# Attention scores of the first block: second product over 128 rows, keys' low parts kept in the gate rows' buffers

## Chip, cores and metric

One core of a Trainium2 chip runs the whole program in one launch. The metric is the device time of that core in microseconds (us); lower is better. All times of instructions are from one profiled execution of the kernel before.

## What is computed

Two transformer blocks are run one after the other on 256 latent tokens and 256 context tokens of width 1024. The change is in the first block, which has two layers. Each layer is: a feed-forward sublayer, an attention sublayer, a second feed-forward sublayer. Layer 0 has neighbourhood attention (16 heads of 64, each query sees a window of latent keys and all 256 context keys; the context queries are computed too). Layer 1 has windowed attention with 16 query heads on 4 key heads and a sink logit, for latent queries only. What matters here is the product of queries and keys:

```
s_win = jnp.einsum('bcqhd,bicjhd->bhcqij', q_r, k_r).astype(jnp.float32) + bias
s_ctx = jnp.einsum('bcqhd,bkhd->bhcqk', q_r, kc).astype(jnp.float32)
p = jax.nn.softmax(jnp.concatenate([s_win, s_ctx], axis=-1), axis=-1)
```

with head dimension 64 and 512 keys (256 latent, 256 context).

## The kernel before

Products keep nearly full float32 precision by splitting each operand into a high part (rounded to the fast fp32r type) and a low part (what the rounding left). A projection is three products into one accumulator, at lines 247, 248 and 249 (`mm3`): high by high, high by low, low by high.

Two heads of 64 share the 128 rows (partitions) of one projected tile; a head's rows are `ROWS[j]` (line 842). `head_parts` (line 845) makes the operands of the scores from such a tile. For the queries it makes one tile per head: the head's own 64 rows hold the high part (ScalarE, line 861), the other head's 64 rows hold this head's low part (VectorE, line 867). For the keys it makes one tile per head with the high part twice, once in each half (ScalarE, lines 861 and 864), and one tile `lo` for both heads with the low parts, each head on its own 64 rows (VectorE, line 865).

`attend_rows` (line 871) computes the scores; its `dot` is two matmuls into one PSUM bank: line 878 over all 128 rows, which is (query high + query low) by key high, and line 879 over the head's 64 rows alone, which is query high by key low. A head pair of layer 0 has four such dots against 512 keys (latent queries) and four against 256 keys (context queries), with 8 head pairs; a pair of layer 1 has four dots against 512 keys, again with 8 pairs. That makes 64 + 32 = 96 dots.

After the scores come `softmax_rows` (line 788: VectorE maximum at lines 805, 810 and 815, ScalarE exponential at 819, VectorE scaling at 828), `transpose_probs` (line 832: TensorE transposes at 838, ScalarE copies at 839) and the product with the values at line 914, whose output tile is 64 columns wide per head, so that its matmuls use the array as 128 rows by 64 columns.

`neighborhood` (line 944) goes over head pairs: project the next pair's queries and keys (`project_qk`, 48 matmuls), finish the current pair (`finish`: transposes and values), score the next (`score`). `window` (line 1054) does the same with queries alone (24 matmuls a pair, `project_tile`), since its two key tiles are made once; there each projected tile goes through a rotation (`roped`, line 1076) first. Instructions are written in this order per engine; a scheduler at build time interleaves them where they don't depend on each other, and each engine then runs its own list strictly in order.

The gate rows: `gate_rows` (line 443) loads a row of 1024 numbers, spread over 128 partitions, into the buffers `gate0` (latent) and `gate1` (context), by two DMAs of GpSimd's queue (line 449). The last reader before attention is the residual of the feed-forward sublayer (line 569); `close_attention` (line 1032) loads the next gates for the residual after attention. Both buffers idle between. In layer 1 only `gate0` is loaded by `close_attention`, since the context isn't needed any more.

`e.zeros` (line 358) is a tile of 256 columns of zeros that is there already.

Of the kernel before, what the change touches and what calls it, by code (L numbers as in the profile page):

```python
# [11 lines left out]
F32R = mybir.dt.float32r  # L12
BF16 = mybir.dt.bfloat16
AF = mybir.ActivationFunctionType
ALU = mybir.AluOpType
AX = mybir.AxisListType.X

P = 128
D = 1024
KT = D // P  # L20
NT = 512
HALF = 256
# [819 lines left out]
ROWS = [slice(0, 64), slice(64, 128)]  # L842


def head_parts(e, pool, src, tag, scale, keys, bufs=1):

    V, S, nm = e.V, e.S, e.nm
    n = int(src.shape[-1])

    def tile(i):
        return pool.tile([P, n], F32R, tag=f"{tag}{i}", bufs=bufs, name=nm("hp"))

    hi = [tile(j) for j in range(2)]
    lo = tile(2) if keys else None
    for j in range(2):
        r, o = ROWS[j], ROWS[1 - j]  # L860
        S.activation(hi[j][r], src[r], AF.Copy, scale=scale)
        h = hi[j][r].bitcast(F32)
        if keys:
            S.copy(hi[j][o], hi[j][r])
            V.tensor_tensor(lo[r], src[r], h, ALU.subtract)
        else:
            V.scalar_tensor_tensor(hi[j][o], src[r], scale, h, ALU.mult, ALU.subtract)  # L867
    return hi, lo


def attend_rows(e, pool, q, k, bias, sinks, with_ctx):

    T = e.T
    kh, kl = k

    def dot(b, j, qc, kc):
        r = ROWS[j]
        T.matmul(b, q[j][:, qc], kh[j][:, kc], start=True, stop=False)  # L878
        T.matmul(b, q[j][r, qc], kl[r, kc], start=False, stop=True)  # L879

    lat, sk = [], []
    for j in range(2):
        for qt in range(2):
            b = e.bank("S")
            dot(b, j, slice(qt * P, qt * P + P), slice(0, NT))
            lat.append((b, bias(j, qt)))
            sk.append(sinks(j) if sinks else None)
    jobs = [(softmax_rows(e, pool, lat, sk if sinks else None), 0, 4)]
    if with_ctx:
        ctx = []  # L890
        for j in range(2):
            b = e.bank("S").rearrange("p (a b) -> p a b", a=2)
            for qt in range(2):
                c0 = HALF + qt * P
                dot(b[:, qt], j, slice(c0, c0 + P), slice(HALF, NT))
                ctx.append((b[:, qt], None))
        jobs.append((softmax_rows(e, pool, ctx), 2, 2))
    return jobs
# [21 lines left out]
def head_outputs(e, pool, n, last):  # L920

    oh, ol = e.uh_ul
    kept = pool.tile([P, last, n], F32, name=e.nm("kept"))

    def split(k, o):
        e.S.activation(oh[:, k, :n], o, AF.Copy)
        e.V.tensor_tensor(ol[:, k, :n], o, oh[:, k, :n].bitcast(F32), ALU.subtract)  # L930

    def take(k, o):
        if k < last:
            e.V.tensor_copy(kept[:, k], o)
            return
        if k == last:
            for i in range(last):
                split(i, kept[:, i])
        split(k, o)

    return take


def neighborhood(e, rest):
    nc, a, V, S, G, T, nm, per = e.nc, e.a, e.V, e.S, e.G, e.T, e.nm, e.per
    uh, ul = e.uh_ul
    with ExitStack() as st:
        pool = e.pool(nm("na"), st)
        take = head_outputs(e, pool, NT, KT - 2)

        def lhs(k, t):
            return uh[:, k, t * P : t * P + P], ul[:, k, t * P : t * P + P]

        def values(dh):
            v = [pool.tile([P, 512], F32, tag=f"v{t}", name=nm("v")) for t in range(4)]
            e.project(
                e.wunits(a["nav"][dh], KT, 2), lhs, range(4),
                lambda t, y: S.copy(v[t], y),
            )
            return v  # L960

        vals, qks, rows = {}, {}, {}

        def qk_weights(hp):
            return [
                e.split(e.raw(a["naqk"][hp, :, i * D : (i + 1) * D], (KT, P)))
                for i in range(2)
            ]

        def products(b, w, c):  # L970
            for k in range(KT):
                e.mm3(b[:, c], w[0][:, k], w[1][:, k], uh[:, k, c], ul[:, k, c],
                      k == 0, k == KT - 1)

        def close_qk(hp, bs):
            q = head_parts(e, pool, bs[0], "q", 0.125, False)[0]
            qks[hp] = q, head_parts(e, pool, bs[1], "k", 1.0, True)

        def project_qk(hp):
            ws = qk_weights(hp)  # L980
            bs = [e.bank("B") for _ in range(2)]
            for i in range(2):
                products(bs[i], ws[i], slice(0, NT))
            close_qk(hp, bs)

        def score(hp):
            bt = e.fb[0].tile([P, 2, 2, HALF], F32, tag=f"lnr{hp % 2}", name=nm("nab"))
            for rq in range(4):
                nc.scalar.dma_start(
                    bt[64 * (rq % 2) : 64 * (rq % 2) + 64, rq // 2],  # L990
                    a["nabias"][:, 2 * hp : 2 * hp + 2, 3 - rq : 7 - rq],
                )
            q, k = qks.pop(hp)
            rows[hp] = attend_rows(e, pool, q, k, lambda j, qt: bt[:, qt, j], None, True)

        def finish(hp):
            o = e.bank("O")
            attend_values(
                e, rows.pop(hp), vals[hp // 4],
                lambda j: slice((2 * (hp % 4) + j) * 64, (2 * (hp % 4) + j) * 64 + 64), o,  # L1000
            )
            take(hp, o)

        lead = []
        for hp in range(2):
            ws = qk_weights(hp)
            bs = [e.bank("L") for _ in range(2)]
            for i in range(2):
                products(bs[i], ws[i], slice(0, HALF))
            lead.append((ws, bs))  # L1010
        for hp, (ws, bs) in enumerate(lead):
            for i in range(2):
                products(bs[i], ws[i], slice(HALF, NT))
            if hp == 0:
                close_qk(0, bs)
        vals[0] = values(0)
        rest()
        score(0)
        for hp in range(KT):
            if hp == 0:  # L1020
                close_qk(1, lead[1][1])
            elif hp + 1 < KT:
                project_qk(hp + 1)
            if hp == 4:
                vals[1] = values(1)
            finish(hp)
            if hp + 1 < KT:
                score(hp + 1)
    return close_attention(e, 0, a["nao"], uh, ul, range(4))
# [24 lines left out]
def window(e, rest):  # L1054
    nc, a, V, S, G, T, nm, per = e.nc, e.a, e.V, e.S, e.G, e.T, e.nm, e.per
    uh, ul = e.uh_ul
    with ExitStack() as st:
        pool = e.pool(nm("wa"), st)
# [17 lines left out]
        def roped(b, n):  # L1076
            t = e.dn[0].tile([P, NT], F32, tag="rt", bufs=2, name=nm("roped"))[:, :n]
            S.copy(t, b[:, :n])
            rb = e.bank("R")
            T.matmul(rb[:, :HALF], rot, t[:, :HALF], start=True, stop=True)  # L1080
            tmp = pool.tile([P, HALF], F32, tag="rtmp", bufs=2, name=nm("rtmp"))
            V.tensor_tensor(tmp, rb[:, :HALF], rope[:, 1], ALU.mult)
            V.tensor_tensor(t[:, :HALF], t[:, :HALF], rope[:, 0], ALU.mult)
            V.tensor_tensor(t[:, :HALF], t[:, :HALF], tmp, ALU.add)
            return t

        ks, qs, rows = [], {}, {}

        def tile_weights(m):
            on = G if m >= 4 else V  # L1090
            return e.split(e.raw(a["waqk"][m // 2, :, (m % 2) * D : (m % 2 + 1) * D], (KT, P)), on)

        def products(b, w, c):
            for k in range(KT):
                e.mm3(b[:, c], w[0][:, k], w[1][:, k], uh[:, k, c], ul[:, k, c],
                      k == 0, k == KT - 1)

        def project_tile(m):
            w = tile_weights(m)
            b = e.bank("B")  # L1100
            products(b, w, slice(0, HALF))
            qs[m - 2] = head_parts(e, pool, roped(b, HALF), "q", 0.125, False, 2)[0]

        def score(i):
            rows[i] = attend_rows(
# [12 lines left out]
        lead = {}  # L1118
# [3 lines left out]
        for m in range(2):  # L1122
            w, b = lead[m]
            products(b, w, slice(HALF, NT))
        for m in range(2):
            qs[m] = head_parts(e, pool, roped(lead[2 + m][1], HALF), "q", 0.125, False, 2)[0]
        e.project(e.wunits(a["wav"], KT, 4), lhs, range(4), evac)
        rest()
        for m in range(2):
            ks.append(head_parts(e, pool, roped(lead[m][1], NT), f"k{m}", 1.0, True))  # L1130
        score(0)
        for i in range(KT - 2):
            project_tile(i + 4)
# [695 lines left out]
```

## Time and profile before

| | |
|---|---|
| three runs, median (lowest to highest) | 2608.67 us (2604.34 to 2611.02) |
| profiled execution, own time | 2611.17 us |
| its span, first to last instruction | 2609.0 us |
| TensorE busy | 2437.8 us (93%) |
| VectorE, ScalarE, GpSimd busy | 1677.8 (64%), 834.6 (32%), 138.1 (5%) us |
| mean granted clock of TensorE | 0.976 |

Busy is the time in which an engine has an instruction in work. TensorE's matmuls are pipelined and their ends are modelled: a matmul that starts while the one ahead is still in work is shown overlapping it, so what tells the pace is the time from one start to the next. A matmul comes with a load of its stationary operand (LDWEIGHTS, shown as engine PEld).  A shape such as 64*128 behind a matmul is the part of the array that it uses, rows by columns.

### The profile page before, as it was taken

The page shows a single profiled execution, that of the slowest core. Times are in us where ns is not written, and L with a number is a line of the kernel's source. Part 1 is how long each engine was busy: PE and PEld are TensorE (multiplying, and loading weights), DVE is VectorE, ACT ScalarE, POOL GpSimd, SP SyncE. Part 2 cuts the span into 40 slices and gives each one's busy share as a digit, 9 for nine tenths or more (in the row PEclk, how much of TensorE's full clock was granted, in tenths as well). Part 3 has the DMA queues.
Part 4 walks back from the last instruction along what each step waited for, and adds up shares of the span by engine and source line. Part 5 has one row for each costly group of instructions (what it writes and reads, how often), then busy time and mean ns, then how long its engine had stood idle before and what let it go on. Part 6 is the DMA issues. An engine that isn't in the chain of part 4 may idle for free.

```text
span 2609.0 us, 33471 instructions
## 1 busy us (share of the span) xinstructions
PE 2437.8 (93%) x12930; PEld 1772.0 (68%) x12930; DVE 1677.8 (64%) x3134; ACT 834.6 (32%) x1412; POOL 138.1 (5%) x151
## 2 busy tenths in 40 slices
PE   8999999999999999999999998999998999798865
PEld 5888888676888888888887768997665422455211
DVE  5978856645899764997985778877744322564211
ACT  3322224645322221322222564444432100443000
POOL 0000000000000000000000200001101000210000
PEclk9999999999999999999999999999998999998987
DMA  8766623222277763576653326875127899536998
GB/s 322 265 198 201 192 77 115 65 81 96 93 253 243 240 227 122 179 235 200 216 180 101 95 81 208 303 235 170 51 81 296 343 427 422 201 104 253 428 427 337
DMA packets 118847, 545.46 MB, mean 209 GB/s; under 512 B 15008, under 2 KB 21408, under 8 KB 106656
## 3 DMA queue, kind: packets, MB, share of 16 engines
q1 hardware_dynamic: 104256, 517.25, 55.5%
q10 hardware_dynamic: 10368, 12.37, 1.6%
q0 software_dynamic: 4064, 13.70, 1.5%
q8 instruction: 102, 1.67, 0.3%
q14 instruction: 57, 0.47, 0.1%
HBM read 542.15 MB, written 1.11 MB: 208 GB/s over the span
## 4 chain that ended last, share of the span: by engine, by line
PE 80%; DMA 7%; DVE 7%; ACT 2%; POOL 2%; issue 2%; ACTq 0%; SPq 0%; POOLq 0%; DVEq 0%
PE pB L247 12%; PE pB L248 12%; PE pB L249 12%; PE pA L249 7%; PE pA L247 7%; PE pA L248 7%; PE pA L1534 5%; DMA big<-in_mgu 3%; DMA big<-in_mdn 3%; PE pB L1580 2%; PE pO L914 2%; PE pT L838 2%; PE pS L879 1%; PE pS L878 1%; PE pX L1781 1%
## 5 line engine op out<-in xcount | busy, mean ns | idle before, releaser
L461 ACT ACTIVATE w<-raw 128x1024 fp32r<-128x1024 f32 (+1 forms) x360 | 372.4, 1036 | 671.1 <-PE pA L249 368.2
L248 PE MATMUL pB<-ul,w 128*128 128x512 f32 (+1 forms) x1616 | 576.5, 357 | 0.0
L247 PE MATMUL pB<-uh,w 128*128 128x512 f32 (+1 forms) x1616 | 573.6, 357 | 2.0 <-DVE hp L867 1.4
L249 PE MATMUL pB<-uh,w 128*128 128x512 f32 (+1 forms) x1616 | 575.2, 356 | 0.2 <-DVE w L463 0.2
L463 DVE TENSOR_TENSOR w<-raw,w 128x1024 fp32r<-128x1024 f32 (+1 forms) x352 | 421.5, 1200 | 208.0 <-ACT w L461 207.5
L384 DVE CUSTOM_DVE_ANT_0 junk<-modw,cb,bmod 128x1024 bf16<-128x1024 f32 x384 | 491.9, 1281 | 7.7 <-DMA modw<-in_wmodd 2.3
L247 PEld LDWEIGHTS pB<-uh,w 128*128 128x128 f32 x1616 | 305.2, 189 | 49.0 <-issue 1.8
L249 PEld LDWEIGHTS pB<-uh,w 128*128 128x128 f32 x1616 | 305.5, 189 | 47.5 <-issue 3.5
L248 PEld LDWEIGHTS pB<-ul,w 128*128 128x128 f32 x1616 | 305.7, 189 | 45.3 <-issue 2.7
L247 PE MATMUL pA<-w,gh 128*128 128x512 f32 x616 | 242.6, 394 | 0.0
L249 PE MATMUL pA<-w,gl 128*128 128x512 f32 x616 | 241.4, 392 | 0.0
L248 PE MATMUL pA<-w,gh 128*128 128x512 f32 x616 | 240.6, 391 | 0.0
L1534 PE MATMUL pA<-big,xs 128*32 128x512 f32 x1536 | 187.8, 630 | 33.7 <-DMA big<-in_mgu 33.7
L247 PE MATMUL pA<-w,uh 128*128 128x512 f32 (+2 forms) x416 | 158.0, 380 | 0.0
L248 PE MATMUL pA<-w,uh 128*128 128x512 f32 (+2 forms) x416 | 156.7, 377 | 0.0
L249 PE MATMUL pA<-w,ul 128*128 128x512 f32 (+2 forms) x416 | 156.3, 376 | 0.0
L1534 PEld LDWEIGHTS pA<-big,xs 128*32 128x32 f32 x1536 | 48.0, 113 | 156.8 <-issue 102.0
L249 PEld LDWEIGHTS pA<-w,gl 128*128 128x128 f32 x616 | 115.7, 188 | 25.6
L247 PEld LDWEIGHTS pA<-w,gh 128*128 128x128 f32 x616 | 115.7, 188 | 24.9 <-issue 0.2
L248 PEld LDWEIGHTS pA<-w,gh 128*128 128x128 f32 x616 | 115.7, 188 | 24.3
L653 ACT ACTIVATE sa<-pB 128x512 f32<-128x512 f32 (+1 forms) x88 | 48.1, 546 | 258.9 <-PE pB L249 258.9
L1580 PE MATMUL pB<-big,hT 128*32 128x512 f32 x768 | 100.0, 617 | 20.6 <-DMA big<-in_mdn 15.7
(301 smaller groups left out, 2819.9 us busy)
## 6 DMA issues: line engine op xcount, KB each, us to landing
big<-in_mgu SPq DMA_DIRECT2D x64, 2048.0 KB, 17.2
modw<-in_wmodd SPq DMA_DIRECT2D x224, 512.0 KB, 4.5
raw<-in_ffin SPq DMA_DIRECT2D x176, 512.0 KB, 4.8
big<-in_mdn SPq DMA_DIRECT2D x30, 2048.0 KB, 17.7
raw<-in_ffout SPq DMA_DIRECT2D x80, 512.0 KB, 4.5
wm<-in_wmodp SPq DMA_DIRECT2D x16, 512.0 KB, 6.5
gate<-gscr POOLq DMA_DIRECT2D x16, 512.0 KB, 5.0
raw<-in_naqk SPq DMA_DIRECT2D x16, 512.0 KB, 3.7
```

Source lines behind the costliest of these rows:

```text
L247: T.matmul(o, lh, rh, start=start, stop=False)
L248: T.matmul(o, lh, rl, start=False, stop=False)
L249: T.matmul(o, ll, rh, start=False, stop=stop)
L384: V.tensor_tensor_reduce(out=junk, in0=w, in1=cb[(b, v)], scale=1.0, scalar=bmod[:, ci, j : j + 1], op0=ALU.mult, op1=ALU.add, accum_out=m ...
L461: S.activation(hi, src, AF.Copy)
L463: sub = on.tensor_tensor(lo, src, hi.bitcast(F32), ALU.subtract)
L653: S.activation(sa[:, :n], pa[:, :n], AF.Silu)
L838: T.transpose(b[:, kb], p[:, kb * P : kb * P + P], e.ident)
L878: T.matmul(b, q[j][:, qc], kh[j][:, kc], start=True, stop=False)
L914: T.matmul(o[rs[j], c], v[k0 + kb][:, vcol(j)], pts[j][:, kb], start=kb == 0, stop=kb == nkb - 1, tile_position=(0, 64 * j),)
L1534: T.matmul(pg[v][i][32 * ex : 32 * ex + 32], xs[(v, k // 2)][:, k % 2, c : c + 32], wv[:, ex, i], start=k == 0, stop=k == KT - 1, tile_pos ...
L1580: T.matmul(py[v][32 * ex : 32 * ex + 32], hT[v][:, f, 32 * ex : 32 * ex + 32], wv[:, f2, ex], start=f == 0, stop=f == 3, tile_position=(0, ...
```

## The change

- For the queries, `head_parts` makes a third tile, `both`: one ScalarE activation over all 128 rows, the high parts of both heads. It is 512 columns in layer 0, 256 in layer 1.
- For the keys, the low parts of each head go into a tile of their own with 128 rows (`lows[j]`), whose rows of the other head are zeros. The VectorE subtraction at line 865 is the same, with another place to write to. These tiles are two halves of a gate row's buffer: `gate0` in layer 0, `gate0` and `gate1` for the two key tiles of layer 1. `low_keys` writes the zeros with ScalarE copies of 64 rows by 256 columns: four per buffer, once for a whole layer.
- The second product of a dot then takes all 128 rows of `both` and of `lows[j]`.

```diff
-def head_parts(e, pool, src, tag, scale, keys, bufs=1):
+def head_parts(e, pool, src, tag, scale, keys, bufs=1, lows=None):
...
     hi = [tile(j) for j in range(2)]
-    lo = tile(2) if keys else None
     for j in range(2):
         r, o = ROWS[j], ROWS[1 - j]
         S.activation(hi[j][r], src[r], AF.Copy, scale=scale)
         h = hi[j][r].bitcast(F32)
         if keys:
             S.copy(hi[j][o], hi[j][r])
-            V.tensor_tensor(lo[r], src[r], h, ALU.subtract)
+            V.tensor_tensor(lows[j][r], src[r], h, ALU.subtract)
         else:
             V.scalar_tensor_tensor(hi[j][o], src[r], scale, h, ALU.mult, ALU.subtract)
-    return hi, lo
+    if keys:
+        return hi, lows
+    both = tile(2)
+    S.activation(both, src, AF.Copy, scale=scale)
+    return hi, both
+
+
+def low_keys(e, n, i):
+
+    both = e.per.tile([P, 2, n], F32R, tag=f"gate{i}", name=e.nm("low"))
+    lows = []
+    for j in range(2):
+        t = both[:, j]
+        o = ROWS[1 - j]
+        for c in range(0, n, HALF):
+            e.S.copy(t[o, c : c + HALF], e.zeros[o])
+        lows.append(t)
+    return lows
...
-    kh, kl = k
+    (q, both), (kh, kl) = q, k
 
     def dot(b, j, qc, kc):
-        r = ROWS[j]
         T.matmul(b, q[j][:, qc], kh[j][:, kc], start=True, stop=False)
-        T.matmul(b, q[j][r, qc], kl[r, kc], start=False, stop=True)
+        T.matmul(b, both[:, qc], kl[j][:, kc], start=False, stop=True)
...
         vals, qks, rows = {}, {}, {}
+        lows = low_keys(e, NT, 0)
...
-            q = head_parts(e, pool, bs[0], "q", 0.125, False)[0]
-            qks[hp] = q, head_parts(e, pool, bs[1], "k", 1.0, True)
+            q = head_parts(e, pool, bs[0], "q", 0.125, False)
+            qks[hp] = q, head_parts(e, pool, bs[1], "k", 1.0, True, lows=lows)
...
-            ks.append(head_parts(e, pool, roped(lead[m][1], NT), f"k{m}", 1.0, True))
+            ks.append(head_parts(
+                e, pool, roped(lead[m][1], NT), f"k{m}", 1.0, True, lows=low_keys(e, NT, m)
+            ))
```

The other two calls of `head_parts` in `window` only lose their `[0]`.

## Rows read from the trace of the kernel before

**Rows 1.** The page: the chain that ended last, share of the span by engine.

```profile
PE 80%; DMA 7%; DVE 7%; ACT 2%; POOL 2%; issue 2%; ACTq 0%; SPq 0%; POOLq 0%; DVEq 0%
```

**Rows 2.** Busy time in the two attention stages (layer 0, then layer 1).

```profile
446.00:634.00 188.00, 185.62 (x853) 125.80 (x851) 110.46 (x302) 108.68 (x242) 2.72 (x5) 1.00 0.24 77
...
1469.00:1548.00 79.00, 78.00 (x407) 50.81 (x408) 63.71 (x247) 54.11 (x125) 1.14 (x2) 0.98 0.10 32
```

**Rows 3.** Line 879, the second product, whole run: forms, and its idle time.

```profile
L879 PE MATMUL pS<-hp,hp x96: 379/492/503, 446.7 to 1546.8; 64*128 64x512 f32 x64, 64*128 64x256 f32 x32
...
  issue: 17.9, 67
```

**Rows 4.** Timeline of TensorE, layer 1's end: start us, duration us.

```profile
1545.65 0.39 PE L249 MATMUL pB<-w,ul 128*128 128x512 f32 x1
1545.97 0.49 PE L879 MATMUL pS<-hp,hp 64*128 64x512 f32 x1
1546.39 0.50 PE L878 MATMUL pS<-hp,hp 128*128 128x512 f32 x1
1546.82 0.50 PE L879 MATMUL pS<-hp,hp 64*128 64x512 f32 x1
1547.25 0.50 PE L249 MATMUL pB<-w,ul 128*128 128x512 f32 x1
1547.59 0.39 PE L247 MATMUL pB<-w,uh 128*128 128x512 f32 x1
```

**Rows 5.** The same view: a first product of the scores with no second behind it.

```profile
1544.16 0.50 PE L878 MATMUL pS<-hp,hp 128*128 128x512 f32 x1
1544.50 0.40 PE L247 MATMUL pB<-w,uh 128*128 128x512 f32 x1
1544.73 0.39 PE L248 MATMUL pB<-w,uh 128*128 128x512 f32 x1
```

**Rows 6.** TensorE, layer 0: dots against 256 keys, and 256-column projection matmuls.

```profile
450.72 0.38 PE L879 MATMUL pS<-hp,hp 64*128 64x256 f32 x1
451.04 0.38 PE L878 MATMUL pS<-hp,hp 128*128 128x256 f32 x1
...
399.74 0.28 PE L247 MATMUL pL<-uh,w 128*128 128x256 f32 x1
399.86 0.28 PE L248 MATMUL pL<-ul,w 128*128 128x256 f32 x1
```

**Rows 7.** TensorE: the value product next to a second product, first and last place.

```profile
490.06 1.08 PE L914 MATMUL pO<-pt,v 128*64 128x256 f32 x6
...
1542.29 1.08 PE L914 MATMUL pO<-pt,v 128*64 128x256 f32 x8
```

**Rows 8.** Timeline of all engines, layer 0: a projection matmul and the next weight load.

```profile
444.33 0.39 PE L247 MATMUL pA<-w,uh 128*128 128x512 f32 x1
444.34 0.19 PEld L248 LDWEIGHTS pA<-w,uh 128*128 128x128 f32 x1
```

**Rows 9.** ScalarE: the query and key activations, and the activations of one head pair.

```profile
L861 ACT ACTIVATE hp<-pB x24: 591/593/597, 464.3 to 623.1; 64x512 fp32r<-64x512 f32 x24
L861 ACT ACTIVATE hp<-roped x20: 400/413/631, 1452.6 to 1534.7; 64x256 fp32r<-64x256 f32 x16, 64x512 fp32r<-64x512 f32 x4
...
526.38 0.59 ACT L861 ACTIVATE hp<-pB 64x512 fp32r<-64x512 f32 x1 [3.29 <-PE pB L249]
```

**Rows 10.** ScalarE's timeline ahead of layer 1's attention: its idle time, in brackets.

```profile
1441.10 1.93 ACT L490 ACTIVATE u<-pU,affh,affs 128x256 f32<-128x256 f32 x4 [8.31 <-PE pU L482]
```

**Rows 11.** Layer 0: gates' last reads before attention, first reads after it, last score.

```profile
L569 DVE SCALAR_TENSOR_TENSOR rt<-pA,gate x5: 679/682/691, 369.7 to 399.6; 128x512 f32<-128x512 f32 x5
...
L569 DVE SCALAR_TENSOR_TENSOR rt<-pA,gate x8: 672/684/692, 660.7 to 690.5; 128x512 f32<-128x512 f32 x8
...
633.66 0.38 PE L879 MATMUL pS<-hp,hp 64*128 64x256 f32 x1
```

**Rows 12.** VectorE in a cycle of layer 1: the wait ahead of the head's output copy.

```profile
1511.04 0.42 DVE L934 COPY kept<-pO 128x256 f32<-128x256 f32 x1 [2.03 <-PE pO L914]
```

More of the change, by code (lines that the diff above doesn't have):

```diff
@@ L1101, in project_tile @@
             products(b, w, slice(0, HALF))
-            qs[m - 2] = head_parts(e, pool, roped(b, HALF), "q", 0.125, False, 2)[0]
+            qs[m - 2] = head_parts(e, pool, roped(b, HALF), "q", 0.125, False, 2)
         def score(i):
@@ L1125, in window @@
         for m in range(2):
-            qs[m] = head_parts(e, pool, roped(lead[2 + m][1], HALF), "q", 0.125, False, 2)[0]
+            qs[m] = head_parts(e, pool, roped(lead[2 + m][1], HALF), "q", 0.125, False, 2)
         e.project(e.wunits(a["wav"], KT, 4), lhs, range(4), evac)
```

## The prediction

> **What bounds the kernel now.** I read the page first: TensorE holds 80% of the chain that ended last [rows 1]. That is a mean over stages, so next I read the two stages in which the scores are computed. In both TensorE is busy nearly without a break, 185.6 of 188 us and 78.0 of 79 us, at a granted clock of 1.00 and 0.98, while VectorE has 110 and 64 us and ScalarE 109 and 54 us in them [rows 2]. A busy TensorE need not be one at its peak, so the third view is the line of the second product: 96 matmuls on 64 rows, with 17.9 us of idle time put down to "issue", that is, to nothing that another engine did [rows 3]. The timeline then shows what that is. In a stream of full-array matmuls of 512 columns one starts every 0.23 us. The step into a 64-row product takes 0.32, and in a row of alternating products every step takes 0.42 or 0.43; the step out takes 0.43, and the one after it still 0.34 [rows 4]. With 256 columns a step beside a 64-row product is 0.32 us against 0.12 us for full-array matmuls [rows 6].
>
> Is it the 64 rows? The first product reads the same kind of tiles into the same kind of bank, and where a projection follows it directly, the second step behind it is 0.23 us as in any stream [rows 5] (the first, 0.34, still has the change from a value product that ran ahead of it, as the last step of rows 4 has one). So neither the score's tiles nor its bank make the wait; what changes at the slow steps is the shape of the array in use. The weight load tells the same: the next full-array load starts 0.01 us after a full-array matmul has started, beside it [rows 8], whereas 67 loads of 64 rows stood idle first, 17.9 us in all [rows 3].
>
> **Part 1, the second product over 128 rows.** The number of matmuls stays, their columns stay. What goes is the change of shape on either side of the second product. 96 products have 192 sides. I went through the timeline for each: at 18, 12 in layer 0 and 6 in layer 1, the neighbour is a value product on 128*64 [rows 7], the first and the last of the 18. There a change of shape stays, so these gain nothing. 174 sides remain, 116 in layer 0 and 58 in layer 1. The price of a side is 0.43 − 0.23 = 0.20 us at 512 columns [rows 4] and 0.32 − 0.12 = 0.20 at 256 [rows 6]. An isolated product gives nearly the same: 0.09 in, 0.20 out and 0.11 on the next step, 0.40 for two sides [rows 4]. So 174 × 0.20 = 34.8 us of TensorE's time, 23.2 in layer 0 and 11.6 in layer 1.
>
> A rule speaks against it. The Trainium skill, "TensorE: Matmul & The Clock Gate", section "The mechanism", says that a weight load overlaps with a matmul in flight only if it goes to other row groups; by that the wider load would have to wait just as well, and part 1 would be worth nothing. The trace disagrees, with a full load 0.01 us behind the start of a full matmul [rows 8].
>
> **Part 2, `both`.** Sixteen more ScalarE activations. The nearest rows are the same activation on half the partitions, 0.593 us for 512 columns and 0.41 for 256 [rows 9]; I take these, since the columns are the same: 8 × 0.59 + 8 × 0.41 = 8.0 us. In layer 0 the query's bank is complete one 24-matmul projection (24 × 0.23 = 5.5 us) ahead of the key's, and ScalarE then idles 3.29 us before the key's first activation [rows 9], which covers 0.59. In layer 1 ScalarE has 25 us free in 79 [rows 2], but the activation stands at the end of a short chain from rotation to score. If the last second product of each of the 16 head pairs waits for it, that costs 0.4 each, 16 × 0.4 = 6.4 us. Bounds: 0 and 8.0; nothing makes it a gain. I take 6, for this and other small waits that come to light once TensorE runs faster, because each engine runs its list in order.
>
> **Part 3, the zeros.** Twelve copies of 64 by 256 at 0.4 us [rows 9], 4.8 us. They need the gates' last reads, which end with the residual at 399.6 + 0.7 us in layer 0 [rows 11], and they stand in the lists ahead of the attention, where ScalarE idles 8.31 us in layer 1 [rows 10] and in layer 0 in the same place. I take 0; without that cover it is 4.8.
>
> **Part 4, the buffers.** The first load of the next gates must now wait for the last score of layer 0, 633.7 + 0.4 us, and stands so long at the head of GpSimd's queue, with the second gate's load and a row load of the layer norm behind it. The first reader comes at 660.7 [rows 11]: 26 us are there for three loads. Cost 0; a cost begins where they take longer than that. In layer 1 `gate0` holds the first key tile, whose last score is the fourth of eight; nothing is late. The subtractions for the low parts keep count and size.
>
> **Sum.** 34.8 − 6 = 28.8 us. The profiled execution, 2611.2 us (its span plus 2.2), would become 2582.4. It stands 2.5 above the median of 2608.7, so I forecast 2580 on the scale of the medians. What follows the attention stages is moved as a whole, since it waits for TensorE and its loads for buffers, not for a time.
>
> **Rivals.**
> - *Half is given back.* With 11.6 / 8 = 1.5 us less per cycle in layer 1, VectorE is next: 63.7 of 79 us busy [rows 2], and its idle time per cycle is a wait of about 2 us for the value product [rows 12]. If the loop of softmax, transposes and values sets the cycle there, the 11.6 us are lost, and if the same takes a third of layer 0's 23.2, 15.5 us are left: 2593. For it: VectorE at 81%. Against: TensorE hardly waits for anyone now.
> - *The step stays slow.* If a load does wait for the rows in use, or the wait belongs to a second product for another reason, the gain is 0, and of parts 2 and 3 between nothing and the 4.8 us of the zeros shows behind an equally busy TensorE: 2609 to 2614, no change. The trace speaks against it [rows 5, 8]. This is where the rule quoted under part 1 would lead (the Trainium skill, the same page and section).
> - *Slower, by ScalarE in the chain.* If TensorE waited for ScalarE in every pair (queries, `both`, keys, then the score), the freed time would turn into waits and all of parts 2 and 3 would be in the open: 8.0 + 4.8 = 12.8 us, 2621. It decides once those waits take more than the 34.8 us freed. Against: ScalarE idles 3.3 us in that very place [rows 9], and TensorE's idle time is 2.4 us in 188 [rows 2].
>
> **How the numbers follow.** Forecast 0.72, half given back 0.18, no change 0.06, slower 0.04. A measurement here tells about 0.3%, or 7.8 us, from no change. The first two cases are faster by more: 0.90; same 0.06; slower 0.04. The range starts from the whole of part 1 with nothing given back (2574), less 4 us, as the lowest run (2604.3) lies below the median: 2570. It ends between the second case and the third, at 2598, where 10 us of gain are left.
>
> **What would show it.** Line 879 reads 128*128; its step from the line ahead is 0.23 us at 512 columns, 0.12 at 256, and its idle time under "issue" is nearly gone, except beside line 914. The stretch from first to last score shrinks by some 20 us in layer 0 and 8 to 11 in layer 1; feed-forward stages keep their length. Sixteen activations of 128 rows and twelve copies are new on ScalarE, in former idle time. I am wrong if steps into line 879 stay at 0.3 to 0.4 us, if TensorE waits for ScalarE's query activations by over 10 us in all, or if the stages shrink and a later one grows.

## The result, and the profile after

The changed kernel takes 2585.36 us (median of four runs, 2582.49 to 2586.65) where the kernel before, run beside it, takes 2609.85 (four runs, 2604.34 to 2617.82): a ratio of 0.9894, 95% interval 0.9878 to 0.9910, or 24.5 us less. Its profiled execution took 2585.48 us, with a span of 2583.6, 25.4 below that of before. TensorE is busy for 2410.5 us instead of 2437.8, and the engines' shares of the chain that ended last have hardly moved (compare [rows 1]):

```profile
PE 79%; DVE 8%; DMA 7%; ACT 2%; POOL 2%; issue 2%; SPq 0%; POOLq 0%; ACTq 0%; DVEq 0%
```

The second product is now line 896 (first product 895, value product 931, transposes 838, their copies 839; query high part 862, query low part 868, `both` 872, key copy 865, zeros 884). Its group over the whole run, against [rows 3]:

```profile
L896 PE MATMUL pS<-low,hp x96: 275/392/796, 449.4 to 1525.1; 128*128 128x512 f32 x64, 128*128 128x256 f32 x32
...
  issue: 3.8, 10
```

The array is used whole, and the idle time put down to "issue" fell from 17.9 us to 3.8. The timeline of TensorE at the first dots of layer 0 (start us, duration us) shows the steps:

```profile
450.11 0.39 PE L895 MATMUL pS<-hp,hp 128*128 128x512 f32 x1
450.34 0.39 PE L896 MATMUL pS<-low,hp 128*128 128x512 f32 x1
...
451.83 0.28 PE L895 MATMUL pS<-hp,hp 128*128 128x256 f32 x1
451.95 0.28 PE L896 MATMUL pS<-low,hp 128*128 128x256 f32 x1
```

From start to start it is 0.23 us at 512 columns and 0.12 at 256, where [rows 4, 6] had 0.42 and 0.32. Every one of these matmuls brings a full load of its own; a rule by which such a load waits for the rows in use would not allow 0.12 us (the Trainium skill, "TensorE: Matmul & The Clock Gate", section "The mechanism", has this rule in its list of what overlaps; the measurement differs from it, and fits the paragraph at the head of that section, by which a load for the background weight buffer is pulled ahead too).

Where the time went is read from two marks per layer. The second product's group, layer 0 and then layer 1, gives the first and the last start:

```profile
L896 PE MATMUL pS<-low,hp x64: 275/386/796, 449.4 to 622.8; 128*128 128x512 f32 x32, 128*128 128x256 f32 x32
...
L896 PE MATMUL pS<-low,hp x32: 388/396/628, 1457.5 to 1525.1; 128*128 128x512 f32 x32
```

Layer 0's stretch is 173.4 us, against 187.0 before (446.7 in [rows 3] to 633.66 in [rows 11]): 13.6 less. Layer 1's is 67.6 against 77.0 (1469.85 to 1546.82): 9.3 less. The whole layer-1 stage runs from the ninth to the last of the 18 instructions of line 583 (GpSimd, layer norm); the group of that line and its ninth instruction, before and then after:

```profile
L583 POOL TENSOR_TENSOR mv<-mv,halfneg x18: 550/904/1537, 384.4 to 1584.9; 128x1 f32<-128x1 f32 x18
...
1042.66 1.45 POOL L583 TENSOR_TENSOR mv<-mv,halfneg 128x1 f32<-128x1 f32 x2 [223.93 <-DVE mv L582]
```

```profile
L583 POOL TENSOR_TENSOR mv<-mv,halfneg x18: 548/903/1532, 387.2 to 1562.9; 128x1 f32<-128x1 f32 x18
...
1031.18 1.44 POOL L583 TENSOR_TENSOR mv<-mv,halfneg 128x1 f32<-128x1 f32 x2 [223.42 <-DVE mv L582]
```

The account of the 25.4 us, by these marks: up to the first layer norm +2.8 (387.2 against 384.4, a part that the change doesn't touch); from there to layer 0's last score −13.7; from that score to the layer-1 stage −0.6; the layer-1 stage −10.5 (531.7 against 542.2); from there to the end −3.4. The first and the last of these differ by as much or more between executions of kernels that are the same there: over the profiles of this study the first part took 383.6 to 387.9 us, the last 1016.0 to 1027.1.

So layer 1 gave what was expected and layer 0 gave less: "some 20 us" were forecast there. Part of what stands in the way is one place, at the scores of the third head pair (the expectations below call it the second). The busy time of all engines in 470 to 492 us (columns: window, its length, then busy us of PE, PEld, DVE, ACT, POOL with counts, granted clock, DMA share, GB/s), before and then after:

```profile
470.00:492.00 22.00, 20.39 (x105) 11.51 (x104) 12.45 (x38) 15.16 (x40) 0.00 (x0) 1.00 0.17 50
```

```profile
470.00:492.00 22.00, 17.51 (x88) 11.28 (x87) 14.04 (x46) 14.57 (x39) 0.00 (x0) 0.84 0.26 79
...
472.00:476.00 4.00, 1.78 (x11) 0.95 (x9) 3.52 (x11) 2.81 (x7) 0.00 (x0) 1.00 0.56 185
476.00:480.00 4.00, 2.24 (x10) 1.42 (x9) 3.42 (x11) 3.95 (x15) 0.00 (x0) 0.78 0.01 4
480.00:484.00 4.00, 3.50 (x12) 2.29 (x12) 1.51 (x3) 3.09 (x6) 0.00 (x0) 0.50 0.00 0
484.00:488.00 4.00, 4.00 (x24) 2.66 (x25) 1.68 (x8) 0.72 (x3) 0.00 (x0) 0.87 0.37 102
```

TensorE stands idle for 4.5 us of 22 instead of 1.6, most of it between 473.6 and 480, and behind that its granted clock is 0.50, the lower of its two levels, 1.2 instead of 2.4 GHz. The timeline of TensorE names what it waited for (in brackets: idle us ahead of the instruction, and what ended it):

```profile
473.30 0.28 PE L896 MATMUL pS<-low,hp 128*128 128x256 f32 x1
475.81 0.47 PE L895 MATMUL pS<-hp,hp 128*128 128x512 f32 x1 [2.22 <-DVE hp L868]
477.71 1.53 PE L838 MATMUL pT<-ident,prob 128*128 128x128 f32 x8 [1.43 <-DVE prob L828]
478.89 0.78 PE L895 MATMUL pS<-hp,hp 128*128 128x512 f32 x1
480.50 1.12 PE L838 MATMUL pT<-ident,prob 128*128 128x128 f32 x4 [0.83 <-ACT pt L839]
```

and VectorE's timeline shows why line 868 was late:

```profile
473.19 0.69 DVE L951 COPY kept<-pO 128x512 f32<-128x512 f32 x1 [0.41 <-PE pO L931]
473.80 0.16 DVE L817 TENSOR_SCALAR sm<-sm 128x4 f32<-128x4 f32 x1
473.86 1.08 DVE L815 TENSOR_REDUCE sm<-pS 128x1 f32<-128x256 f32 x3
474.98 0.68 DVE L868 SCALAR_TENSOR_TENSOR hp<-pB,hp 64x512 fp32r<-64x512 f32 x1
```

VectorE had hardly any idle time from 473.19 to 475.7 us: the query's low part stood in its list behind the current pair's softmax. TensorE had nothing to put between: in the changed kernel's order, made at build time, no projection matmul (lines 247 to 249) starts from 463.9 to 491.4 us, while the kernel before has five between 472 and 484 alone (four, if the window is counted from the start of layer 0's stretch). The first product that starts behind the waits, at 478.89, lasts 0.78 us in the timeline, where it is 0.39 in the stream above.

The waits on layer 0 as a whole, TensorE first and then its weight loads (us in total, times, longest):

```profile
PE pS L895 <- DVE hp L868: 2.2, 1, 2.2
PE pT L838 <- ACT pt L839: 1.8, 2, 1.0
PE pT L838 <- DVE prob L828: 1.4, 1, 1.4
...
PEld pT L838 <- ACT pt L839: 8.7, 21, 1.3
```

The loads of the transposes waited 3.5 us in 9 places for ScalarE's copy in the kernel before; now it is 8.7 us in 21. Such a wait of a load can lie beside a matmul in work and is then no loss of TensorE's time; whether it was one, the experiment "sides alone" tells.

The zeros and the buffers show no cost of their own, as forecast. ScalarE's timeline has the four copies of layer 0 in idle time:

```profile
384.50 1.44 ACT L884 CAST low<-zeros 64x256 fp32r<-64x256 f32 x4 [15.29 <-DVE rt L569]
```

The gates' loads stand in GpSimd's timeline at 620.07 and 623.71 us, on either side of the last score's start (622.78), and their first reader comes at 649.3.

### The profile page after: what moved, and what is told of

Read it like the earlier page. It is cut to its first block, busy times and chain, and to the rows that moved or that the text cites. A ratio compares the mean times of both kernels' runs of the same rounds, so it can differ in the third digit from the quotient of the medians.

```text
span 2583.6 us, 33502 instructions
## 1 busy us (share of the span) xinstructions
PE 2410.5 (93%) x12930; PEld 1767.3 (68%) x12930; DVE 1675.4 (65%) x3134; ACT 844.2 (33%) x1440; POOL 137.2 (5%) x151
## 4 chain that ended last, share of the span: by engine, by line
PE 79%; DVE 8%; DMA 7%; ACT 2%; POOL 2%; issue 2%; SPq 0%; POOLq 0%; ACTq 0%; DVEq 0%
PE pB L247 12%; PE pB L248 12%; PE pB L249 12%; PE pA L247 7%; PE pA L249 7%; PE pA L248 7%; PE pA L1554 5%; DMA big<-in_mgu 3%; DMA big<-in_mdn 3%; PE pB L1600 2%; PE pO L931 2%; PE pT L838 2%; DVE w L463 1%; PE pX L1801 1%; PE pU L482 1%
```

## The experiments

All ratios are to the kernel before, run beside them on the same chip: 2610.86 us (median) for the first four kernels, 2612.66 for the next four, 2610.55 for the last two. "Layer 0's stretch" is the time from the first to the last start of the second product there: 187.0 us before, 173.4 after. A program that changes one line is given a new order by the scheduler in most of these kernels; where TensorE's list is the changed kernel's own, the text says so.

### Rows alone: 128 rows without `both`, zeros and new buffers

```diff
 (against the kernel before)
-        T.matmul(b, q[j][r, qc], kl[r, kc], start=False, stop=True)
+        T.matmul(b, q[j][:, qc], kl[:, kc], start=False, stop=True)
```

> The kernel before with one edit: the second product takes all 128 rows of tiles that are there already (the head's query tile and the shared tile of low key parts). No both, no zeros, no gate buffers. It computes something else in the low-order part, since the other head's rows are added. Main theory (the price is the change of array shape, 0.20 us on each side that has no value product beside it): about 170 sides, 34 us, less small waits: 2578 (2574 to 2583), faster than the changed kernel's 2585, and every step into the second product at 0.23 (512 columns) or 0.12 us (256). On the 5.8 us that TensorE waited in layer 0's second head pair after the change: if the cause is ScalarE's extra activation, the wait is under 2 us here; if it is the order of the list, which here too puts the next pair's projection ahead of that pair's scores, 3 us or more stay. Rival (the side work costs nothing, and the gain is simply smaller per side, 24.5/169 = 0.145): 2585, like the changed kernel.

Measured: 2587.51 us (2584.37 to 2588.92), ratio 0.9913 [0.9899, 0.9928]. The time missed the main theory's 2578 and its range, and lies nearer to the 2585 of the rival, by which a side is worth less. The steps are as the main theory has them, 0.23 and 0.12 us; the group of layer 0 and the window of the bad place:

```profile
L879 PE MATMUL pS<-hp,hp x64: 278/338/501, 449.5 to 619.3; 128*128 128x512 f32 x32, 128*128 128x256 f32 x32
...
470.00:492.00 22.00, 19.35 (x99) 12.48 (x99) 15.07 (x46) 16.37 (x42) 0.00 (x0) 0.92 0.18 55
```

The stretch is 169.8 us, 17.2 below before, and TensorE is idle for 2.65 us in the window. The edit takes no instruction and adds none, and yet the order made at build time came out another, with some of the hole in it. So a one-line edit here is never one thing alone; what `both` costs can't be read from this kernel.

### Sides alone: everything of the change but the 128 rows

```diff
 (against the changed kernel)
-        T.matmul(b, both[:, qc], kl[j][:, kc], start=False, stop=True)
+        T.matmul(b, both[ROWS[j], qc], kl[j][ROWS[j], kc], start=False, stop=True)
```

> The changed kernel with one edit: the second product takes the head's own 64 rows of both and of its low tile, so all side work stays (both, zeros, buffers), and TensorE's list is the same instruction by instruction. Main theory: 169 sides without a value product beside them come back at 0.20 us, 33.8 us, of which some 3 hide in the waits of layer 0's second head pair: 2616 (2612 to 2620), 2 to 10 us slower than the kernel before, which is the price of both and its order. Rival (a side is worth 0.145 us, and side work and order cost nothing): 2610, same as before.

Measured: 2616.30 us (2613.04 to 2622.01, seven runs), ratio 1.0027 [1.0016, 1.0039]. TensorE's list is that of the changed kernel, instruction for instruction, so this pair isolates the shape. The groups of layer 0 and layer 1, and the window:

```profile
L896 PE MATMUL pS<-low,hp x64: 377/391/686, 447.9 to 639.6; 64*128 64x512 f32 x32, 64*128 64x256 f32 x32
L896 PE MATMUL pS<-low,hp x32: 491/496/792, 1476.0 to 1553.5; 64*128 64x512 f32 x32
...
470.00:492.00 22.00, 18.15 (x83) 10.55 (x78) 13.36 (x39) 13.70 (x35) 0.00 (x0) 0.84 0.23 73
...
PEld pT L838 <- ACT pt L839: 4.6, 10, 1.3
```

Two prices follow. The rest of the change, without its benefit, costs 2616.30 − 2610.86 = 5.4 us (4 to 10 by the interval of the ratio), nearly all of it in layer 0 (stretch 191.7, 4.7 above before; layer 1 77.5, 0.6 above), and the hole with its low clock is there already. And the 128 rows alone are worth 18.3 us in layer 0 (191.7 to 173.4) and 9.9 in layer 1 (77.5 to 67.6). By the marks of line 583 it is 11.3 in layer 1, but 1.2 us of that lie ahead of the first second product, where the two kernels do the same. (In layer 1's stretch the granted clock is 0.956 in sides alone and 0.975 in the changed kernel, so a little of the 9.9 may be the clock's; in layer 0 it is 0.98 in both.)

In the changed kernel 23 sides stand next to a value product, 17 of them in layer 0, so 169 sides gain. At 0.20 us that would be 22.2 us and 11.6; measured it is 0.17 us a side, in either layer, between the 0.20 of the main theory and the rival's 0.145. Since the lists are the same, every step from one start to the next can be compared with itself. In layer 0 the whole difference lies at the steps into and out of the second product (16.9 us) and the steps right behind those (1.6); over all the other steps, those into a transpose among them, it is less than 0.2 us in sum. So the longer waits of the transposes' loads (4.6 us here, 8.7 in the changed kernel) took little of the gain: at most the 1.3 us that the ten steps from a second product of 512 columns to a transpose fall short of 0.20 each.

What falls short is the price of some sides. Of the 164 steps into and out of the second product inside the two stretches, 108 are shorter by 0.15 us or more, 44 by 0.05 to 0.15, and 12 by less. Of the 44, 20 stand one place behind a value product. An example from layer 1, the changed kernel and then sides alone:

```profile
1492.28 1.94 PE L931 MATMUL pO<-pt,v 128*64 128x256 f32 x14
1494.15 0.50 PE L895 MATMUL pS<-hp,hp 128*128 128x512 f32 x1
1494.48 0.40 PE L896 MATMUL pS<-low,hp 128*128 128x512 f32 x1
```

```profile
1517.86 1.94 PE L931 MATMUL pO<-pt,v 128*64 128x256 f32 x14
1519.73 0.49 PE L895 MATMUL pS<-hp,hp 128*128 128x512 f32 x1
1520.15 0.50 PE L896 MATMUL pS<-low,hp 64*128 64x512 f32 x1
```

The step into line 896 is 0.33 us against 0.42: the change of shape at the value product is still in it, so 0.09 is gained and not 0.20.

### `both` first: high parts made once, own rows copied

```diff
 (against the changed kernel; both's activation at the end is gone)
+    if not keys:
+        both = tile(2)
+        S.activation(both, src, AF.Copy, scale=scale)
     for j in range(2):
         r, o = ROWS[j], ROWS[1 - j]
-        S.activation(hi[j][r], src[r], AF.Copy, scale=scale)
-        h = hi[j][r].bitcast(F32)
+        h = (hi[j] if keys else both)[r].bitcast(F32)
         if keys:
+            S.activation(hi[j][r], src[r], AF.Copy, scale=scale)
...
         else:
             V.scalar_tensor_tensor(hi[j][o], src[r], scale, h, ALU.mult, ALU.subtract)
+            S.copy(hi[j][r], both[r])
```

> The changed kernel with both made first, by one activation over 128 rows ahead of the others, the low part taken from it, and the head's own rows of the query tile copied from it on ScalarE (which reads SBUF, not the bank that VectorE is reading). The scheduler then leaves some projection matmuls between the parts of layer 0's second head pair. Theory of the order: the 5.8 us of waits in that pair fall under 2 us, and the time is 2580 (2577 to 2583). Theory of ScalarE's load (the activation itself is what is late): no gain, 2585 (2583 to 2588), since ScalarE has the same work. Main theory on the price of a side: steps into the second product stay at 0.23 and 0.12 us.

Measured: 2583.79 us (2578.21 to 2586.33), ratio 0.9899 [0.9881, 0.9918]. The time falls in the range of the theory of ScalarE's load and just outside that of the theory of the order; the second set of runs, below, lies in the order's range. In layer 0 the hole is smaller, though not under the 2 us that the theory of the order had, and the clock is whole.

```profile
L898 PE MATMUL pS<-low,hp x64: 275/388/502, 449.3 to 616.6; 128*128 128x512 f32 x32, 128*128 128x256 f32 x32
...
470.00:492.00 22.00, 19.42 (x107) 12.94 (x107) 16.24 (x52) 16.83 (x48) 0.00 (x0) 1.00 0.18 55
```

The stretch is 167.3 us, 6.1 below the changed kernel's. The layer-1 stage is 529.3 us against 531.7; the marks place the difference behind layer 1's last score (35.5 us to the end of the stage against 37.7).

### `both` on GpSimd

```diff
 (against the changed kernel)
-    S.activation(both, src, AF.Copy, scale=scale)
+    for j in range(2):
+        e.G.tensor_copy(both[ROWS[j]], hi[j][ROWS[j]])
```

> The changed kernel with both copied by GpSimd from the two query tiles, two copies of 64 rows, so that ScalarE has no more work than before except for the zeros. The list still has no projection matmuls in layer 0's second head pair behind its first transposes. Theory of the order: the waits there stay at 4 us or more, 2585 (2583 to 2588). Theory of ScalarE's load: they fall under 2 us, 2580 (2577 to 2583). A slow GpSimd copy (over 2 us) would show as a wait of TensorE for it ahead of the second product, in every pair, and then the time is above 2588.

Measured: 2582.49 us (2582.12 to 2586.37), ratio 0.9899 [0.9884, 0.9914].

```profile
L897 PE MATMUL pS<-low,hp x64: 276/388/502, 449.0 to 617.1; 128*128 128x512 f32 x32, 128*128 128x256 f32 x32
...
470.00:492.00 22.00, 19.66 (x104) 12.82 (x103) 17.44 (x52) 16.14 (x44) 1.24 (x2) 1.00 0.23 73
```

The theory that the order alone makes the hole had 4 us or more of waits stay; 2.3 us stayed, at a whole clock, so it missed. The theory of ScalarE's load had them fall under 2 us; the time is in its range, the waits are just above. Here TensorE waits 0.4 us for line 868 instead of 2.2: the low part comes earlier, and no projection matmul stands in the hole either. Taking `both` out of ScalarE's list, in which it waits for line 868 in three places, 3.2 us in all, goes with that; but the list of TensorE is in another order here too, so how much is due to ScalarE's time and how much to the order is not shown.

### The hole filled, the changed kernel again, and the two versions again

Ten matmuls of 512 columns are put ahead of the first dot of the third head pair (the one with the hole), into a bank that the dot then starts anew:

```diff
 (against the changed kernel)
+            for _ in range(fill if j == 0 and qt == 0 else 0):
+                T.matmul(b, e.uh_ul[0][:, 0, :P], e.uh_ul[0][:, 0], start=True, stop=True)
...
-            rows[hp] = attend_rows(e, pool, q, k, lambda j, qt: bt[:, qt, j], None, True)
+            rows[hp] = attend_rows(
+                e, pool, q, k, lambda j, qt: bt[:, qt, j], None, True, 10 if hp == 2 else 0
+            )
```

> The changed kernel with ten more matmuls of 512 columns, whose result is overwritten, in the place where TensorE waits 2.5 us for VectorE in layer 0's second head pair; otherwise TensorE's list is the same. Theory of the clock: after that wait the granted clock is 0.50 for some 6.5 us in the changed kernel; with TensorE kept at work it stays at 1.00, and the stretch from layer 0's first to its last score is 2 to 3 us shorter than the changed kernel's 173.6, although 2.3 us of work were added: 2583 (2580 to 2586) in all. Rival (the clock's fall is a matter of chance, or costs nothing since TensorE waits there anyway): the stretch is the same or up to 2.3 us longer, 2585 to 2588.

> The changed kernel itself, on the same chip as the others of this call: 2585 (2582 to 2588), ratio 0.989 to 0.991, and again about 0.84 of granted clock between the first scores and the end of layer 0's second head pair (it is the same in the run with the 64-row product, which has the same list). If it reads 1.00 here, the fall of the clock is chance.

Measured: 2587.39 us with the filling (2584.61 to 2588.37), ratio 0.9895 [0.988, 0.991]; 2589.15 for the changed kernel again (2586.56 to 2591.18), ratio 0.9903 [0.9888, 0.9918]. In time they can't be told apart. The stretch can, since TensorE's list is otherwise the same: 171.7 us filled, 173.3 and 173.4 in the two profiles without. The filled kernel's group, windows and timeline:

```profile
L896 PE MATMUL pS<-low,hp x64: 275/390/505, 450.0 to 621.8; 128*128 128x512 f32 x32, 128*128 128x256 f32 x32
...
472.00:476.00 4.00, 4.00 (x21) 2.84 (x21) 2.99 (x9) 2.81 (x8) 0.00 (x0) 1.00 0.68 235
476.00:480.00 4.00, 2.24 (x13) 1.26 (x11) 3.39 (x11) 3.98 (x16) 0.00 (x0) 1.00 0.02 6
480.00:484.00 4.00, 2.88 (x15) 1.74 (x15) 2.19 (x6) 3.58 (x7) 0.00 (x0) 1.00 0.00 0
...
474.04 2.47 PE L903 MATMUL pS<-uh 128*128 128x512 f32 x10
476.43 0.47 PE L895 MATMUL pS<-hp,hp 128*128 128x512 f32 x1
478.33 1.12 PE L838 MATMUL pT<-ident,prob 128*128 128x128 f32 x8 [1.43 <-DVE prob L828]
```

The wait for line 828 is the same 1.43 us, but no wait stands ahead of it, and the granted clock is 1.00 throughout. With ten matmuls more, 2.47 us in the timeline, the stretch is 1.6 us shorter. Compared step by step, the difference arises between 478.4 and 485.3 us, where the changed kernel has the low clock: 2.1 us of shorter steps, 0.5 of it given back in longer waits. So some 1.6 us are what the low clock had cost, less than the 2 to 3 of the expectation, and too little to be seen in the time, which lies in the rival's range. That the fall of the clock is more than chance is borne out by the changed kernel again and sides alone, which have 0.84 in the same window too.

> The kernel with both made first, again, in more rounds. By its trace the two attention layers gained 32.7 us against 24.4 of the changed kernel; the rest of the run differed by a few us from execution to execution. Theory (the gain in the two layers is passed on): 2579 (2576 to 2582). Rival (what is won there is lost behind it): 2584 (2582 to 2586).

> The kernel with both copied by GpSimd, again, in more rounds. By its trace the two layers gained 27.7 us against 24.4 of the changed kernel. Theory: 2582 (2580 to 2584), 3 us faster than the changed kernel of this call. Rival: no difference from it beyond 1.5 us.

Measured: `both` first 2578.47 us (2572.76 to 2579.64), ratio 0.9855 [0.9837, 0.9874]; on GpSimd 2584.79 (2577.18 to 2585.47), ratio 0.9880 [0.9862, 0.9898]. In layer 0 the first again has 167.4 us, so its profile repeats; `both` on GpSimd has 168.0 (445.7 to 613.7). **`both` first beats both kernels:** here each of its runs lies below each of the changed kernel's, 10.7 us by the medians. Over both sets of runs the gap is smaller, a median of 2579.5 for its eight runs against 2586.6 for the changed kernel's eight, 7 us. `both` on GpSimd is 4.4 us below the changed kernel here and 2.9 in the first set, where the runs overlap; its time here lies just above the range expected.

### `both` early, and its copies on GpSimd

The first moves the activation of `both` ahead of the loop and changes nothing else; the second is `both` first, with the copy of the own rows on GpSimd:

```diff
 (against the changed kernel)
+    if not keys:
+        both = tile(2)
+        S.activation(both, src, AF.Copy, scale=scale)
     for j in range(2):
...
-    both = tile(2)
-    S.activation(both, src, AF.Copy, scale=scale)
     return hi, both
```

```diff
 (against "both first")
-            S.copy(hi[j][r], both[r])
+            e.G.tensor_copy(hi[j][r], both[r])
```

> The changed kernel with one move: the activation that makes both stands ahead of the other query activations instead of behind them; nothing else differs (ScalarE's instructions are the same in number and size, and each still reads the projection's bank). Theory of the place (the activation stood in ScalarE's list behind VectorE's read of the same bank, and shifted the lists of layer 0's second head pair): no wait of ScalarE for line 868 at that activation, layer 0 from first to last score 168 us (166 to 170) against 173.6, granted clock 1.00 there, 2580 (2577 to 2583). Rival (the kernel with both first gained because the low parts and the copies no longer read the bank, or by less time in the bank): 172 us or more, 2585 (2583 to 2588).

> The kernel with both first, and the head's own rows of the query tiles copied from it by GpSimd instead of ScalarE (copies of 64 rows, 0.6 us each where GpSimd copied in an earlier run). Theory: layer 0 stays at 167 to 168 us; in layer 1 GpSimd also has weight splits of 2.4 us in its list, behind which the first copies can wait: total 2579 (2576 to 2584), no clear difference from the kernel with both first (2578). Rival (ScalarE's time still counts): 2575 or less. Rival (GpSimd's copy is late for the first product of the score): TensorE waits for it, 2585 or more.

Measured: early 2584.88 us (2579.96 to 2586.34), ratio 0.9901 [0.9886, 0.9916]; copies on GpSimd 2582.99 (2576.15 to 2585.29), ratio 0.9900 [0.9883, 0.9916]. The group of layer 0 and the window, early:

```profile
L897 PE MATMUL pS<-low,hp x64: 276/388/776, 449.4 to 620.3; 128*128 128x512 f32 x32, 128*128 128x256 f32 x32
...
470.00:492.00 22.00, 18.13 (x96) 11.80 (x94) 14.00 (x45) 16.39 (x46) 0.00 (x0) 0.92 0.23 67
```

The stretches are 170.8 us early and 169.5 (447.2 to 616.8) with the copies on GpSimd. Early, much of the hole stays and the time is near the changed kernel's, so making `both` earlier is not enough by itself: the theory of the place missed in time, stretch and clock, and its rival's 172 us were not reached either. Taking the copies off ScalarE brings nothing over `both` first. All kernels side by side (projection matmuls from TensorE's timeline; idle time is 22 us less PE's busy time in 470 to 492; `both` on GpSimd again, whose stretch begins 3.3 us earlier, in windows moved by as much; counted from the start of the stretch, before has 4 such matmuls and copies on GpSimd 5):

| kernel | projection matmuls started in 472 to 484 us | TensorE idle, us | granted clock | layer 0's stretch, us |
|---|---|---|---|---|
| before | 5 | 1.6 | 1.00 | 187.0 |
| sides alone | 0 | 3.9 | 0.84 | 191.7 |
| changed, twice | 0, 0 | 4.5, 4.3 | 0.84, 0.84 | 173.4, 173.3 |
| hole filled | 0, and the ten | 2.9 | 1.00 | 171.7 |
| `both` early | 2 | 3.9 | 0.92 | 170.8 |
| rows alone | 4 | 2.7 | 0.92 | 169.8 |
| copies on GpSimd | 3 | 3.7 | 1.00 | 169.5 |
| `both` on GpSimd, twice | 0, 0 | 2.3, 2.4 | 1.00, 1.00 | 168.1, 168.0 |
| `both` first, twice | 7, 7 | 2.6, 2.6 | 1.00, 1.00 | 167.3, 167.4 |

## Why the prediction was right, and where it was not

**Confirmed.** The cause, the change of the array's shape, and its size in a row of alternating products, 0.20 us a side. The pair of sides alone and the changed kernel has the same list and differs in the rows of the second product alone, and the two stretches differ by 18.3 + 9.9 = 28.2 us (by the medians 30.9, or 27.2 against the changed kernel again; these come from different sets of runs). The Trainium skill, "TensorEngine Tiling (Array Packing)", section "Key Properties", says that a change of the tiling mode drains TensorE; the trace agrees so far as both the step into a 64-row product and the step out of it are slow. Several 64-row products of the same rows in a row were not tried. The rival "the step stays slow" falls with the steps of 0.23 and 0.12 us. Parts 3 and 4 cost nothing that the marks show. In layer 1, forecast 8 to 11, the stretch shrank by 9.3 us and the stage by 10.5, so the rival "half given back", which lets VectorE's loop set layer 1's cycle, falls too. "Slower, by ScalarE in the chain" needed more than 34.8 us of waits; TensorE's own waits in layer 0 grew by 3.3 us (5.4 us in four places, 2.1 in three before).

**Mis-sized: the 34.8 us of part 1, and layer 0's "some 20 us".** Layer 0's stretch gave 13.6. The term that was too large is 174 × 0.20: sides alone measures 28.2 us. Of the 6.6 us too many, 1.0 is the count: I took the neighbours of the kernel before, with 12 sides next to value products in layer 0, and the new order has 17. The rest is the price, 0.17 us on the mean and not 0.20. The rows had a sign of it: behind a value product a step is 0.34 us with no 64-row product near [rows 5], and yet only direct neighbours of value products were taken off the count. Part 2 held in size, 6 us set aside and 5.4 measured, but not in place: spread as 16 × 0.4 over both layers it left 23.2 − 3.2 = 20 for layer 0, while 4.7 us of it lie there, where the window above has one hole, and 0.6 in layer 1. So layer 0 is 18.3 − 4.7 = 13.6 where 23.2 − 3.2 = 20 was forecast, and layer 1 is 9.9 − 0.6 = 9.3 where it was 11.6 − 3.2 = 8.4. That layer 1 came out in its range is in part luck, since two misses nearly cancel there. The whole came out at 24.5 us instead of 28.8.

**What the prediction didn't have at all** is that the order of the lists is made anew. It reasoned as if each instruction kept its place; the projection matmuls that had filled TensorE's waits in that pair stood elsewhere afterwards, and a wait in their place cost the clock as well. Three versions with another order or another engine for `both` show that it needn't be so. The table suggests two ways out of the hole, projection matmuls in it (`both` first) and the low part earlier (`both` on GpSimd); which detail of the work makes the build-time order pick one or the other stays open, since no edit here sets the order by itself. Open too is why `both` first is 2.2 to 2.4 us shorter in layer 1's stage, in both of its profiles. Whether the second block's products on 64 rows gain in the same way was not tried.

## What to carry to other kernels

A matmul on half of the rows was no shorter here than one on all (0.49 and 0.50 us in [rows 4]), and next to full-array matmuls each change of shape cost up to 0.20 us, 0.17 on the mean: where such products alternate, fill the other rows with zeros, if the operand can be made in the shadow of TensorE. Count the sides in the order that will run, not in the one that did, look one place further for other changes of shape, and where a scheduler makes the order, look at the new lists for a place in which TensorE has nothing left between two waits. Then try the side work in another place or on another engine: the same arithmetic, with its high parts made once, took another 7 us off.

## What the runs showed of the hardware that was not expected

A wait of TensorE has a second price. In the changed kernel its granted clock fell, behind a wait of 2.2 us and one of 1.4, from 1.00 to 0.78 in the window of 476 to 480 us and to 0.50 in the next; with the first wait filled by ten matmuls the clock stayed at 1.00 through the same windows, and the stretch became 1.6 us shorter with 2.5 us of more work in it.

The first 385 us, which no edit touches, took 383.6 to 387.9 us from execution to execution, and the granted clock of the first 40 us differs with it: 1.00 in the profile of before, 0.91 in that of after, here in this order:

```profile
0.00:40.00 40.00, 28.24 (x174) 15.49 (x178) 14.18 (x35) 12.09 (x18) 0.19 (x4) 1.00 0.88 331
```

```profile
0.00:40.00 40.00, 27.05 (x153) 14.08 (x153) 13.24 (x31) 11.37 (x16) 0.19 (x4) 0.91 0.85 313
```

In the two kernels TensorE's instructions up to there are the same. The part behind the layer-1 stage differs by up to 11 us. Differences of some us between two profiled spans are therefore no evidence by themselves; layer 0's stretch repeats to 0.1 us (173.4 and 173.3, 167.3 and 167.4, 168.1 and 168.0), layer 1's only to 0.9 (67.8 and 67.0 for `both` first).
